# Three steps of a hybrid attention layer moved in its hand-written order: norms of the second query group, turns of mixer A's values, differences of mixer B's halves

## The chip, the core and the metric

The kernel runs on one core of a Trainium2 chip. The metric is the device time of one execution in microseconds (us). The median of the three runs shown is 924.02 us (921.49, 924.02 and 924.33).

## What is computed

The layer takes 512 tokens of width 2048, with 16 meta tokens ahead of them (528 positions). The reference, cut to what matters:

```python
hn = rmsnorm(h, pre_norm_g)
proj = einsum('bld,dc->blc', hn, w_in)
qa, ka, va, ga, qb, kb, vb, gb = split(proj)
# mixer A: 8 query heads of 128, 2 key/value heads; q and k are normed per head, then turned by rotary angles
q = axial_rope(rmsnorm(heads(qa), q_g)); k = axial_rope(rmsnorm(heads(ka), k_g))
ya = (softmax(q k^T * scale) v) * silu(ga)
# mixer B: 8 heads, a difference of two softmaxes with a distance penalty
a = softmax(s1) - lam * softmax(s2)
yb = rmsnorm(a v, sub_g) * (1 - lambda_init) * silu(gb)
y = einsum('blc,cd->bld', concat(ya, yb), w_out)
out = (h + rmsnorm(y, post_norm_g))[:, 16:]
```

## The kernel before

**Precision.** Operands are fp32. Each is split into a high part (rounded, on ScalarE, `hi`, L334) and a low part (the remainder, on VectorE, `lo`, L337), and a product is three matmuls: high by high, low by high, high by low. Weights come in chunks of 128 by 1024: loaded into `st` (L148), split into `wh` (ScalarE, L155) and `wl` (VectorE, L156), with three buffers for each of the three.

**Stages.** (1) The eight heads of mixer B: their gate, value, key and query projections, each a `dense_T` of two weight chunks, with the attention of the head before woven between the matmuls. (2) Mixer A, with two groups of four query heads. For each group there are a query projection (`queries_A`), one key head (`keys_A`) and one value head (`values`). In the order of the program: keys and values of group 0, queries of group 0, queries of group 1, then keys and values of group 1. The attention of group 0's heads is woven into the second query projection and what follows it. (3) The eight gates of mixer A, with the attention of the heads woven in. (4) The output projection, made of products of sums and differences of token halves.

**Weaving.** `Lanes` writes the order of TensorE (PE) out by hand. It keeps a clock that counts the expected time of the matmuls and transposes issued so far (`mm` charges a matmul of n columns n / 2370 us, with n at least 256). A task is a generator; `yield x` means that it goes on once this clock has advanced by x, and `poll`, called after every three matmuls of a projection, runs at most one due task that issues to PE. The lags are in `LAG`.

**Order on the other engines.** All matmuls, all transposes and the loads through `load` keep the program's order. Instructions of VectorE (DVE), ScalarE (ACT), GpSimd (POOL) and the other DMAs are ordered by the framework when the program is built: it takes what its own model of times finds ready, earlier program positions first, and may so put a ready instruction of a late position into a gap that it expects. The weight splits stand 60 positions forward (`high_priority`, L153). On the chip each engine then takes its instructions in that fixed order.

**The lines that the change and the steps of the prediction touch:**

- `values` (from L380): the projected values, scaled by `rB` into `vf` (L328, buffer tag `tT`, two buffers), are turned on PE by the task `turn`: four transposes into a PSUM tile `tr` (L63), split into `vh` and `vl`, and `LAG["bank"]` = 2.8 later the 16 meta tokens (`vm`). The task starts `LAG["vals"]` = 3.5 after the projection.
- `tr`, with two PSUM buffers in all, also takes the transposes of the probabilities `p` (L447 to 463: two of four blocks, read by `ph` on ACT and `pl` on DVE, and a small one read by `pm`), of queries (`qn`), of keys (`kfA`, `kn`, `km`) and the products with the values (`pv`). A transposition waits on PE until the buffer's last reader is done.
- attention of a head of mixer A: scores into `sc` (one PSUM tile), scaled and copied with the maximum by DVE (L600), exponentials by ACT (L603), reciprocal by DVE (L604), scaling by POOL (L605), then `p_times_v`.
- `queries_A`: four PSUM tiles copied into `qn` (ACT, L704), then the task `turn` (L707 to 713): for each of the four token blocks `head_norm` (four squares with sums on ACT, L622; POOL's `rstd`, L247 and L249; four scalings on DVE, L625) and `rope` (five operations on DVE, L635 to L640, through a tile `t2` with tag `tT`), then `yield LAG["norm"]` = 4.0, for both groups.
- `keys_A`: the keys, copied into `kfA` (ACT, L646, tag `tT`), turned, normed and roped (`kn`, `km`), and turned back (`kh`, `kl`), by the lags 3.5, 2.8, 10.2 and 2.8.
- `half_dead` (L869): at k = 8 of the last gate's projection, when the tiles of x for k below 8 are dead, mixer B's gated outputs are split into the operands of the first two output products: `b0` (first token half) and `t1` (second half minus first half). The halves are loaded by `come` (L862) into `ob` tiles that lie in buffers of the tags `ql`, `f` and `tT`. The four differences are L877; the splits into `ah`, `al` (b0) and `bh`, `bl` (t1) follow.
- `splits` lists the pairs (`wh`, `wl`) of the weight splits as they were written. At `half_dead` two later chunks have been fetched ahead, so `splits[-3]` is the second chunk of the last gate and `splits[-4]` its first.

Of the kernel before, what the change touches and what calls it, by code (L numbers as in the profile page):

```python
# [29 lines left out]


LAG = dict(vals=3.5, bank=2.8, bankA=1.5, bankB=2.5, turnA=1.5, turnB=1.5, pvA=2.6, pvB=4.0, scB=3.0,
           pB=8.0, ss=6.0, qA=2.35, scA=5.4, pA=4.14, rope=10.2, head=3.85, fin=1.35, qn=1.4, norm=4.0)

AHEAD = -60

# [4 lines left out]
class Lanes:  # L41
# [13 lines left out]
    def mm(self, out, lhsT, rhs, start, stop, **kw):  # L55
        n = int(np.prod(rhs.shape[1:]))
        us = max(n, 256) / 2370.0
        if rhs.dtype == F32:
            us = 4 * max(n, 128) / 2370.0
        self._add(self.nc.tensor.matmul(out, lhsT, rhs, start=start, stop=stop, **kw), us)  # L60

    def transpose(self, out, in_, ident):
        self._add(self.nc.tensor.transpose(out, in_, ident), 0.109)  # L63
# [42 lines left out]
def kernel(ctx: ExitStack, tc: tile.TileContext, xT, xn, xm, w_s, w_t, w_q, w_o,  # L106
                             gpre, gq, gk, lams, gsub, gpost, ident_d, cos_d, sin_d, dist_d, out):
    nc = tc.nc
    lanes = Lanes(tc)
# [50 lines left out]
    splits = []  # L160
# [31 lines left out]
    KEYS = [(0, HALF), (HALF, NT)]  # L192
    REAL = [(NM, NT)]

    def three(ps, wh, wl, k, n0, n1):
        mm(ps, wh, xh[k][:, n0:n1], start=(k == 0), stop=False)
        mm(ps, wh, xl[k][:, n0:n1], start=False, stop=False)
        mm(ps, wl, xh[k][:, n0:n1], start=False, stop=(k == KT - 1))
# [4 lines left out]
    def fetch(ahead=2):  # L203
        while todo and len(chunks) <= ahead:
            src = todo.pop(0)
            chunks.append(src() if callable(src) else wload(src))
        return chunks.pop(0)

    def dense_T(segs, pss=None, half=None):

        pss = pss or [pd.tile([P, 512], F32, name="pd", tag="pd") for _ in segs]
        for k0 in range(0, KT, 8):
            wh, wl = fetch()
            for k in range(k0, k0 + 8):
                c = slice((k - k0) * P, (k - k0 + 1) * P)
                for (n0, n1), ps in zip(segs, pss):
                    three(ps[:, :n1 - n0], wh[:, c], wl[:, c], k, n0, n1)
                    lanes.poll()
                if half and k == 8:
                    half()  # L220
        return pss
# [38 lines left out]
    for t in (TT, 0, 1, 2, 3):  # L260
        rows = P if t < TT else NM
        src = xn[t * P:(t + 1) * P, :] if t < TT else xm
        for j in range(2 if t < 2 else 4):

            tag, w = ("pl", "ph")[j % 2], 1024
            if t >= 2:
                tag, w = ("f", "g", "ql")[t - 2], 512
            st = (gp if tag == "g" else ap).tile([P, w], F32, name="xns", tag=tag,
                                                 bufs=2 if t < 2 else 4)[:rows]
# [56 lines left out]
    def halves(pss, dst):  # L326
        for (n0, n1), ps in zip(KEYS, pss):
            nc.vector.tensor_tensor(out=dst[:, n0:n1], in0=ps[:, :n1 - n0], in1=rB[:, n0:n1],  # L328
                                    op=ALU.mult)
# [3 lines left out]
    def hi(dst, src):  # L333
        nc.scalar.activation(dst, src, AF.Copy)  # L334

    def lo(dst, src, h):
        nc.vector.tensor_tensor(out=dst, in0=src, in1=h.bitcast(F32), op=ALU.subtract)  # L337
# [39 lines left out]
            lo(l2[L], qf[U], q2[U])  # L377
        return (q1, l1), (q2, l2)

    def values(pss):  # L380

        vf = ap.tile([P, NT], F32, name="vf", tag="tT")
        halves(pss, vf)
        vh = ap.tile([P, TT, P], F32R, name="vh", tag="vh")
        vl = ap.tile([P, TT, P], F32R, name="vl", tag="vl")
        vm = ap.tile([96, P], F32R, name="vm", tag="vm")
        nc.vector.memset(vm.bitcast(F32), 0.0)

        def turn():
            yield from whole()  # L390
            tr = ptr.tile([P, 512], F32, name="tr", tag="tr")
            for c in range(TT):
                transpose(tr[:, c * P:(c + 1) * P], vf[:, NM + c * P:NM + (c + 1) * P], ident)
            tv = tr.rearrange("p (c d) -> p c d", d=P)
            hi(vh, tv)
            lo(vl, tv, vh)
            yield LAG["bank"]
            yield from whole()
            tr = ptr.tile([P, 512], F32, name="tr", tag="tr")
            transpose(tr[:NM, :P], vf[:, 0:NM], ident)  # L400
            hi(vm[0:NM], tr[0:NM, :P])
            hi(vm[64:64 + NM], tr[0:NM, :P])
            lo(vm[32:32 + NM], tr[0:NM, :P], vm[0:NM])

        return (vh, vl, vm), lanes.spawn(turn(), LAG["vals"])

    def gate(pss, name):
        g = gp.tile([P, SEQ], F32, name=name, tag="g", bufs=4)
# [8 lines left out]
    def whole():  # L417

        while pv_open[0]:
            yield 0.1  # L420
# [196 lines left out]
    def head_norm(raw, n, g, rows=P):  # L617

        ss = ap.tile([P, 4], F32, name="ssh", tag="ssh", bufs=4)
        for i in range(n):  # L620
            jk = ap.tile([P, P], F32, name="jk", tag="jk", bufs=1)
            nc.scalar.activation(jk[:rows], raw[:, i, :], AF.Square, accum_out=ss[:rows, i:i + 1])  # L622
        rstd(ss[:rows, :n], ss[:rows, :n], P, rows)
        for i in range(n):
            nc.vector.scalar_tensor_tensor(out=raw[:, i, :], in0=raw[:, i, :],  # L625
                                           scalar=ss[:rows, i:i + 1], in1=g[:rows], op0=ALU.mult,
                                           op1=ALU.mult)
# [56 lines left out]
    def queries_A(g, before=None):  # L684

        pss = [pd.tile([P, 512], F32, name="pd", tag="pd") for _ in range(TT)]
        for k0 in range(0, KT, 2):
            wh, wl = fetch()

            for k, ts in [(k, h) for h in ((0, 1), (2, 3)) for k in (k0, k0 + 1)]:  # L690
                c = slice((k - k0) * 512, (k - k0 + 1) * 512)
                for t in ts:
                    ts_ = slice(NM + t * P, NM + (t + 1) * P)
                    mm(pss[t], xh[k][:, ts_], wh[:, c], start=(k == 0), stop=False)
                    mm(pss[t], xl[k][:, ts_], wh[:, c], start=False, stop=False)
                    mm(pss[t], xh[k][:, ts_], wl[:, c], start=False, stop=(k == KT - 1))
                    lanes.poll()
        if before:
            before()
        res = []  # L700
        for t in range(TT):
            tag = "ql" if g == 0 else "fr" if t < 2 else "f"
            qn = ap.tile([P, 4, P], F32, name="qn", tag=tag, bufs=2 if tag == "fr" else 4)
            nc.scalar.activation(qn.rearrange("p n d -> p (n d)"), pss[t], AF.Copy,  # L704
                                 scale=rt[:, t:t + 1])
            res.append(qn)

        def turn():
            for t, qn in enumerate(res):
                head_norm(qn, 4, gqB)  # L710
                rope(qn, cosT[:, t:t + 1].broadcast_to([P, 4, 2, 32]),
                     sinT[:, t:t + 1].broadcast_to([P, 4, 2, 32]))
                yield LAG["norm"]

        return res, lanes.spawn(turn(), 0.0)


# [37 lines left out]
    def otile(name, n, dt=F32R):  # L755
        return xtile(name, n, dt)[:, NM:NT]
# [23 lines left out]
    pss = dense_T(KEYS, [sc[:, 0, :], sc[:, 1, :]], spread)  # L780
# [10 lines left out]
    with behind():  # L791
        lambdas()
    v = values(pss)
    with behind():
        gB = [gate(first[2], "gB0")] + [None] * (NH - 1)
# [6 lines left out]
    for h in range(NH):  # L802
# [6 lines left out]
        if h + 1 < NH:  # L809
            if h:  # L810
                weigh(2)
            pss = dense_T(KEYS)
# [8 lines left out]
    def start_heads(grp, qn, q_task, k, v):  # L821
        for h in range(4 * grp, 4 * grp + 4):
            heads[NH + h] = lanes.spawn(attention_A(h, qn, q_task, *k, *v), LAG["qn"],
                                        q_task if h == 0 else heads[NH + h - 1])

    pss = dense_T(KEYS)
    finish_head(NH - 2)
    kA = keys_A(pss)
    vA = values(dense_T(KEYS))

    def zeros():
        finish_head(NH - 1)
# [3 lines left out]
    start_heads(0, *queries_A(0, zeros), kA, vA)  # L836
    second_q = queries_A(1)
    kA = keys_A(dense_T(KEYS))
    start_heads(1, *second_q, kA, values(dense_T(KEYS)))
    assert not steps and not adds  # L840

    NP = TT // 2 * P
# [1 line left out]
    TTv, SUB, ADD = nc.vector.tensor_tensor, ALU.subtract, ALU.add  # L844
# [5 lines left out]
    def split(tiles, src):  # L850
        h, l = tiles
        hi(h, src)
        lo(l, src, h)
# [11 lines left out]
    def two_(t):  # L865
        return t.rearrange("p (i q) -> p i q", i=2)
# [3 lines left out]
    def half_dead():  # L870
        for to, n in ((b0, 0), (t1, 8)):
            for i in range(4):
                st, sd = of_B[2 * i:2 * i + 2]
                to.append([two_(otile(f"{'ab'[n // 8]}{x}{i}", n + 2 * i + j))
                           for j, x in enumerate("hl")])
                if n:
                    TTv(out=sd, in0=st, in1=sd, op=SUB)  # L877
                    st = sd
                split(to[i], st)

# [285 lines left out]
```

## Time and profile before

The profile shows one execution of 921.97 us, whose span from the first to the last instruction is 920.2 us.

| what | value |
|---|---|
| device time, median of 3 | 924.02 us |
| device time of the profiled execution | 921.97 us |
| its span | 920.2 us |
| mean granted TensorE clock | 0.996 |
| busy: PE / DVE / ACT / POOL | 901.2 / 588.4 / 503.4 / 122.0 us |
| DMA | 149.86 MB, mean 163 GB/s |

In the trace group 0's keys and values are projected up to 474.6 us (`vf` of group 0), its queries up to 518 us, the queries of group 1 up to 567.6 us, the keys of group 1 up to 597.6 us and its values up to 617.5 us. The gates follow up to 755 us, and the output projection up to the end.

Times in rows are in us from the span's start, and mean durations in ns where that is said. A row of the timeline has the start, the duration, the engine, the line, the operation, what it writes and reads, and in brackets how long the engine had stood idle before it and who released it. PE's busy time contains the overlap of pipelined matmuls, so its rows are longer than the distance of their starts.

### The profile page before, as it was taken

How to read it: one execution, taken by the hardware profiler on the slowest of the kernel's cores; microseconds unless marked ns; L12 is line 12 of the kernel's file. 1: busy time of each engine (PE TensorE's matmuls, PEld its weight loads, DVE VectorE, ACT ScalarE, POOL GpSimd, SP SyncE). 2: the span in 40 equal slices, each digit the busy share in tenths (PEclk: the TensorE clock that was granted, in tenths of full speed). 3: DMA queues.
4: the chain of work that ended last, by engine and by line, in shares of the span. 5: the costliest groups of instructions: out<-in, count | busy, mean ns of one | idle time of the engine just before them, and what ended most of it. 6: DMA issues, size and time to landing. Idle time of an engine off the chain costs nothing.

```text
span 920.2 us, 14275 instructions
## 1 busy us (share of the span) xinstructions
PE 901.2 (98%) x5450; PEld 798.7 (87%) x5450; DVE 588.4 (64%) x1041; ACT 503.4 (55%) x877; POOL 122.0 (13%) x168
## 2 busy tenths in 40 slices
PE   9999999999999999999999999998999999999995
PEld 8999898998989899898988888887888888888884
DVE  6676675747557485665764464856555565876887
ACT  6564564737455474654753535555556564665452
POOL 0102110210201111111020101321111100000012
PEclk9999999999999999999999999999999999999998
DMA  9837646664848568475223232133122228889784
GB/s 341 286 120 210 173 124 157 184 195 135 224 119 236 134 180 217 119 224 131 80 70 103 76 107 69 47 109 109 62 77 92 63 87 300 274 284 314 251 250 177
DMA packets 52980, 149.86 MB, mean 163 GB/s; under 512 B 7921, under 2 KB 14961, under 8 KB 52529
## 3 DMA queue, kind: packets, MB, share of 16 engines
q1 hardware_dynamic: 48160, 132.18, 42.3%
q0 software_dynamic: 4608, 16.78, 10.6%
q8 instruction: 42, 0.69, 0.3%
q14 instruction: 26, 0.20, 0.1%
q10 hardware_dynamic: 144, 0.01, 0.0%
HBM read 140.55 MB, written 41.94 MB: 198 GB/s over the span
## 4 chain that ended last, share of the span: by engine, by line
PE 87%; DVE 7%; ACT 2%; DMA 2%; issue 1%; POOL 0%; SPq 0%; DVEq 0%; ACTq 0%; POOLq 0%
PE pd L60 58%; PE po L60 14%; PE sc L60 6%; PE pv L60 5%; PE tr L63 4%; DVE wl L156 1%; DVE y L1064 1%; DMA st<-in_w_s_dram 1%; DVE p L600 1%; DMA ob<-oscr 1%; DMA st<-in_w_o_dram 0%; DVE pl L337 0%; ACT p L603 0%; PE ss L60 0%; DVE y L988 0%
## 5 line engine op out<-in xcount | busy, mean ns | idle before, releaser
L60 PE MATMUL pd<-xh,wh 128*128 128x264 f32 (+1 forms) x992 | 333.4, 336 | 0.0
L60 PE MATMUL pd<-xh,wl 128*128 128x264 f32 (+1 forms) x992 | 323.1, 326 | 0.2
L60 PE MATMUL pd<-xl,wh 128*128 128x264 f32 (+1 forms) x992 | 323.0, 326 | 0.0
L155 ACT ACTIVATE wh<-st 128x1024 fp32r<-128x1024 f32 (+2 forms) x159 | 165.6, 1042 | 205.6 <-PE pd L60 81.0
L156 DVE TENSOR_TENSOR wl<-st,wh 128x1024 fp32r<-128x1024 f32 (+2 forms) x159 | 191.2, 1203 | 102.6 <-ACT wh L155 101.6
L60 PEld LDWEIGHTS pd<-xh,wl 128*128 128x128 f32 x992 | 186.4, 188 | 16.7 <-DVE wl L156 0.6
L60 PEld LDWEIGHTS pd<-xh,wh 128*128 128x128 f32 x992 | 186.8, 188 | 11.1 <-ACT wh L155 0.3
L60 PEld LDWEIGHTS pd<-xl,wh 128*128 128x128 f32 x992 | 187.2, 189 | 9.5
L509 ACT ACTIVATE p<-p,mx 128x528 f32<-128x528 f32 x64 | 47.0, 734 | 43.2 <-DVE mx L501 42.9
L63 PE MATMUL tr<-ident,p 128*128 128x128 f32 (+1 forms) x320 | 50.7, 272 | 3.9 <-DVE pl L337 3.1
L337 DVE TENSOR_TENSOR pl<-tr,ph 128x512 fp32r<-128x512 f32 x64 | 43.3, 685 | 16.6 <-ACT ph L334 16.2
L501 DVE CUSTOM_DVE_ANT_0 p<-sc,dist 128x528 f32<-128x528 f32 x64 | 44.8, 700 | 11.5 <-PE sc L60 11.1
L60 PE MATMUL pd<-wh,xh 128*128 128x512 f32 x128 | 51.1, 399 | 0.0
L60 PE MATMUL pd<-wl,xh 128*128 128x512 f32 x128 | 50.0, 390 | 0.0
L60 PE MATMUL pd<-wh,xl 128*128 128x512 f32 x128 | 49.9, 390 | 0.0
L63 PEld LDWEIGHTS tr<-ident,p 128*128 128x128 f32 (+1 forms) x320 | 36.5, 131 | 15.3 <-DVE pl L337 3.7
L334 ACT ACTIVATE ph<-tr 128x512 fp32r<-128x512 f32 x64 | 37.6, 590 | 22.3 <-PE tr L63 21.8
L603 ACT ACTIVATE p<-p,mxA 128x528 f32<-128x528 f32 x32 | 23.5, 735 | 41.4 <-DVE mxA L600 41.4
L516 DVE SCALAR_TENSOR_TENSOR p<-p,c 128x528 f32<-128x528 f32 x32 | 24.5, 766 | 30.8 <-POOL p L514 30.8
L461 POOL TENSOR_SCALAR pm<-pm 32x256 fp32r<-32x256 f32 x32 | 22.8, 712 | 149.1 <-ACT pm L334 148.6
L605 POOL TENSOR_SCALAR p<-p,smA 128x528 f32<-128x528 f32 x32 | 23.1, 722 | 145.7 <-DVE smA L604 110.9
L749 POOL DMA_DIRECT2D ws<-in_w_o_dram x32 | 26.7, 836 | 118.0 <-DMA ws<-in_w_o_dram 64.7
(221 smaller groups left out, 1591.5 us busy)
## 6 DMA issues: line engine op xcount, KB each, us to landing
st<-in_w_t_dram SPq DMA_DIRECT2D x82, 512.0 KB, 4.2
ws<-in_w_o_dram POOLq DMA_DIRECT2D x32, 512.0 KB, 8.4
st<-ws SPq DMA_DIRECT2D x32, 512.0 KB, 4.0
st<-in_w_o_dram SPq DMA_DIRECT2D x24, 512.0 KB, 4.4
ws<-in_w_o_dram SPq DMA_DIRECT2D x16, 512.0 KB, 5.7
ws<-ws SPq DMA_DIRECT2D x16, 512.0 KB, 5.1
st<-in_w_q_dram SPq DMA_DIRECT2D x16, 512.0 KB, 3.5
xs<-in_xT_dram SPq DMA_DIRECT2D x16, 264.0 KB, 5.5
```

The lines of the kernel that those rows point to most:

```text
L60: self._add(self.nc.tensor.matmul(out, lhsT, rhs, start=start, stop=stop, **kw), us)
L63: self._add(self.nc.tensor.transpose(out, in_, ident), 0.109)
L155: splits.append((nc.scalar.activation(wh[:, c], st[:, c], AF.Copy), nc.vector.tensor_tensor(out=wl[:, c], in0=st[:, c], in1=wh[:, c].bitca ...
L156: nc.vector.tensor_tensor(out=wl[:, c], in0=st[:, c], in1=wh[:, c].bitcast(F32), op=ALU.subtract)))
L334: nc.scalar.activation(dst, src, AF.Copy)
L337: nc.vector.tensor_tensor(out=dst, in0=src, in1=h.bitcast(F32), op=ALU.subtract)
L501: nc.vector.tensor_tensor_reduce(out=two(p), in0=sc[:, :, :HALF], in1=two(dist[:, w0:w0 + NT]), scale=-0.125 / slope(h), scalar=3.0e38, op ...
L509: nc.scalar.activation(p2[m], p2[m], AF.Exp, scale=-1.0, bias=mx[:, m:m + 1], accum_out=sm[:, m:m + 1])
L516: nc.vector.scalar_tensor_tensor(out=p2[0], in0=p2[1], scalar=c2, in1=p2[0], op0=ALU.mult, op1=ALU.add)
L603: nc.scalar.activation(p, p, AF.Exp, scale=-1.0, bias=mx, accum_out=sm)
L605: nc.gpsimd.tensor_scalar(out=p, in0=p, scalar1=sm, scalar2=1.0, op0=ALU.mult, op1=ALU.mult)
L749: nc.gpsimd.dma_start(out=dst, in_=src, accum_op=ALU.add)
```

## The change

- Group 1's norms go in steps of 9.0 on the clock of `Lanes` in place of 4.0; group 0's stay at 4.0.
- The values of mixer A, both groups, are turned 7.0 after their projection in place of 3.5; those of mixer B stay at 3.5.
- The four differences of mixer B's halves are put behind the low part of the last gate's first weight chunk in DVE's order.

```diff
-           pB=8.0, ss=6.0, qA=2.35, scA=5.4, pA=4.14, rope=10.2, head=3.85, fin=1.35, qn=1.4, norm=4.0)
+           pB=8.0, ss=6.0, qA=2.35, scA=5.4, pA=4.14, rope=10.2, head=3.85, fin=1.35, qn=1.4, norm=(4.0, 9.0), valsA=7.0)
...
-    def values(pss):
+    def values(pss, lag="vals"):
...
-        return (vh, vl, vm), lanes.spawn(turn(), LAG["vals"])
+        return (vh, vl, vm), lanes.spawn(turn(), LAG[lag])
...
-                yield LAG["norm"]
+                yield LAG["norm"][g]
...
-    vA = values(dense_T(KEYS))
+    vA = values(dense_T(KEYS), "valsA")
...
-    start_heads(1, *second_q, kA, values(dense_T(KEYS)))
+    start_heads(1, *second_q, kA, values(dense_T(KEYS), "valsA"))
...
                 if n:
-                    TTv(out=sd, in0=st, in1=sd, op=SUB)
+
+                    with tc.issue_after(splits[-4][1].ins):
+                        TTv(out=sd, in0=st, in1=sd, op=SUB)
                     st = sd
                 split(to[i], st)
```

## The prediction

> **What bounds the kernel.** I read the page first. TensorE (PE) is busy nearly throughout, so only its gaps can be won: an edit elsewhere pays as far as PE waits less.
>
> ```profile
> span 920.2 us, 14275 instructions
> ...
> PE 901.2 (98%) x5450; PEld 798.7 (87%) x5450; DVE 588.4 (64%) x1041; ACT 503.4 (55%) x877; POOL 122.0 (13%) x168
> ```
>
> Next the busy times by stretches of 20 us (columns: stretch, sum, then busy time of PE, PEld, DVE, ACT, POOL, then PEclk), around the second query group and in the gates.
>
> ```profile
> 580.00:600.00 20.00, 17.92 (x148) 17.27 (x147) 16.78 (x42) 10.06 (x27) 6.10 (x9) 1.00 0.09 28
> 600.00:620.00 20.00, 18.25 (x145) 17.36 (x144) 11.62 (x29) 10.37 (x29) 5.25 (x9) 1.00 0.33 105
> 620.00:640.00 20.00, 17.85 (x103) 14.45 (x101) 12.67 (x24) 8.78 (x18) 3.50 (x4) 1.00 0.31 106
> ...
> 720.00:740.00 20.00, 20.00 (x116) 17.09 (x115) 10.11 (x20) 11.47 (x19) 3.62 (x5) 1.00 0.23 77
> ```
>
> PE loses 2.08, 1.75 and 2.15 us in 580 to 640, while DVE is at its fullest in the first of these; in 720 to 740 it loses nothing. Third, PE's waits from 563 to 645 us in groups (total, times, longest), and the three longest in the timeline:
>
> ```profile
> PE tr L63 <- DVE pl L337: 3.8, 6, 1.8
> PE tr L63 <- DVE kl L337: 1.9, 1, 1.9
> PE tr L63 <- ACT oA L610: 0.5, 1, 0.5
> ...
> 587.48 0.39 PE L63 MATMUL tr<-ident,p 128*32 128x128 f32 x2 [1.79 <-DVE pl L337]
> ...
> 601.16 0.66 PE L63 MATMUL tr<-ident,kfA 128*128 128x128 f32 x4 [0.78 <-DVE pl L337]
> ...
> 624.36 0.66 PE L63 MATMUL tr<-ident,vf 128*128 128x128 f32 x4 [1.85 <-DVE kl L337]
> ```
>
> All are transposes waiting for one of the two `tr` buffers, whose reader is late. Together they are 6.2 us; that is the most that this change can win here.
>
> **The norms in steps of nine.** The wait at 587.48 has this chain (last matmul of the scores, DVE, then ACT, then DVE):
>
> ```profile
> 580.76 0.28 PE L60 MATMUL sc<-kh,qlA 128*128 128x264 f32 x1
> ...
> 582.11 0.35 DVE L625 SCALAR_TENSOR_TENSOR qn<-qn,ssh,gqB 128x128 f32<-128x128 f32 x1 [1.00 <-POOL ssh L249]
> ...
> 584.59 0.70 DVE L600 CUSTOM_DVE_ANT_0 p<-sc,zed 128x528 f32<-128x528 f32 x1
> ...
> 585.39 0.73 ACT L603 ACTIVATE p<-p,mxA 128x528 f32<-128x528 f32 x1 [3.44 <-DVE mxA L600]
> ...
> 586.12 0.57 ACT L334 ACTIVATE ph<-tr 128x512 fp32r<-128x512 f32 x1
> ...
> 586.74 0.69 DVE L337 TENSOR_TENSOR pl<-tr,ph 128x512 fp32r<-128x512 f32 x1
> ```
>
> The scores end at 581.04, but DVE copies them only at 584.59: norm and rope operations stand ahead, one of which holds the line 1.00 us for POOL. The exponential waits for the copy, `ph` stands behind the exponential on ACT, `pl` behind `ph`, and PE behind `pl`. What the four norm steps cost:
>
> ```profile
> L625 DVE SCALAR_TENSOR_TENSOR qn<-qn,ssh,gqB 128x128 f32<-128x128 f32 x16 | 5.2, 366 | 3.3 <-POOL ssh L249 3.3
> ...
> L639 DVE TENSOR_TENSOR qn<-qn,cosT 128x256 f32<-128x256 f32 x8 | 3.1, 414 | 0.0
> L640 DVE TENSOR_TENSOR qn<-qn,t 128x512 f32<-128x512 f32 x4 | 2.8, 690 | 0.1
> L635 DVE SCALAR_TENSOR_TENSOR t<-qn,sinT 128x256 f32<-128x256 f32 x4 | 2.1, 527 | 0.0
> L637 DVE TENSOR_TENSOR t<-qn,sinT 128x256 f32<-128x256 f32 x4 | 1.7, 413 | 0.0
> ...
> L622 ACT ACTIVATE jk<-qn 128x128 f32<-128x128 f32 x16 | 4.9, 308 | 0.4
> ```
>
> That is 14.9 us of DVE, 3.7 a step. Neither number nor size changes, only their places. The task starts when the last query matmul is written, and the keys end here:
>
> ```profile
> 567.64 0.69 ACT L704 ACTIVATE qn<-pd,rt 128x512 f32<-128x512 f32 x1 [1.13 <-PE pd L60]
> ...
> 597.64 0.66 ACT L646 ACTIVATE kfA<-pd 128x264 f32<-128x264 f32 x2
> ...
> 607.25 1.14 DVE L625 SCALAR_TENSOR_TENSOR kn<-kn,ssh,gkB 128x128 f32<-128x128 f32 x4 [3.83 <-POOL ssh L249]
> ...
> 617.48 0.99 DVE L328 TENSOR_TENSOR vf<-pd,rB 128x264 f32<-128x264 f32 x2
> ```
>
> Steps two to four stood at about 572, 576 and 580, all ahead of the scores of 580.15; now they stand at about 577, 587 and 597 (the hand-written clock runs a little short of the trace). At 581 only step two precedes the copy. Without step three's share in 582.11 to 584.59 (its 1.00 of waiting and its scalings, 0.35 and 0.34) and with step two's rope no longer split by it, the copy comes 1.5 to 3 us earlier, and the wait shrinks by as much: between 0 (the later positions are filled in early again) and 1.79; I take 1.5, the lower end of what the line clears. What is late next: step four, once done by 596, falls near 600. It can use the 3.83 us that DVE idles before 607.25, but 601.16 already shows 0.78 of waiting for a `pl`. I charge 0.5 for it (bounds 0 and one more wait like that, 0.78). The four heads that need these queries start after the values, so the end of the task, four steps of nine, some 39 us after 567.6 or about 606, delays nobody: the first of them begins after 617. Cost there 0; without that cover each us late would be one on PE.
>
> **The differences.** The wait at 624.36:
>
> ```profile
> 618.44 0.28 PE L60 MATMUL sc<-kh,qlA 128*128 128x264 f32 x1
> ...
> 620.59 0.69 DVE L877 TENSOR_TENSOR ob<-ob 128x512 f32<-128x512 f32 x1 [2.12 <-DMA ob<-oscr]
> 621.20 0.70 DVE L600 CUSTOM_DVE_ANT_0 p<-sc,zed 128x528 f32<-128x528 f32 x1
> ...
> 622.00 0.74 ACT L603 ACTIVATE p<-p,mxA 128x528 f32<-128x528 f32 x1 [2.03 <-DVE mxA L600]
> ...
> 622.74 0.58 ACT L334 ACTIVATE kh<-tr 128x512 fp32r<-128x512 f32 x1
> ...
> 623.03 0.67 DVE L877 TENSOR_TENSOR ob<-ob 128x512 f32<-128x512 f32 x1
> 623.62 0.68 DVE L337 TENSOR_TENSOR kl<-tr,kh 128x512 fp32r<-128x512 f32 x1
> ```
>
> A difference that is written in the last gate stands here in DVE's order, and waits 2.12 us for its DMA while the scores behind it have been ready since 618.72. Taken away, copy, exponential, `kh` and `kl` all come about 2 us earlier, `kl` ends near 622 in place of 624.2, and the transposes that wanted the buffer at 622.5 don't wait: 1.85 won (bounds 1.2, if `kl` finds DVE at another 0.67 operation, and 1.85). Their new place:
>
> ```profile
> L877 DVE TENSOR_TENSOR ob<-ob x4: 673/686/693, 620.6 to 632.9; 128x512 f32<-128x512 f32 x4
> ...
> 725.15 1.23 DVE L156 TENSOR_TENSOR wl<-st,wh 128x1024 fp32r<-128x1024 f32 x1
> ...
> 733.10 1.22 DVE L156 TENSOR_TENSOR wl<-st,wh 128x1024 fp32r<-128x1024 f32 x1 [2.04 <-ACT wh L155]
> ...
> 739.58 0.69 DVE L560 TENSOR_TENSOR gt<-pd,rB 128x512 f32<-128x512 f32 x1 [1.87 <-PE pd L60]
> ...
> 745.13 0.62 ACT L334 ACTIVATE bh<-ob 128x512 fp32r<-128x512 f32 x1
> ```
>
> The last gate's first chunk is the `wl` of 725.15 (its buffer is freed three chunks ahead of its use at 739). Four times 0.69, 2.8 us, must fit between there and 745, where their first reader stands; the data came 100 us before, so nothing waits behind them for a DMA. DVE is free for half of 720 to 740 (10.11 busy of 20). I take 0; the other end is one operation ahead of a `pl`, 0.69. The DMAs stay unmoved. If that cover failed, the output products that need the splits start after 755, a reserve of 10 us.
>
> **The values.** Turning them 3.5 later changes PE's order, not its amount. At 624.36 the four transposes come right after those of `kn` and `p`; later, they find the buffers freer. With the differences gone there is little left to win, and the places around have waits of 0.3 to 0.8. I take 0, from -0.5 to 0.78. Their later end frees a `tT` buffer some 3 us later, for which the last `ob` load waits in SP's queue; the weight load behind it serves a chunk some 14 us ahead of its use (as 725.15 stands to 739.58), so this is covered. Group 0's values, turned near 480, are costed the same way: 0.
>
> **The sum.** 1.5 + 1.85 - 0.5 = 2.85 won, and 0.4 of the 1.2 that four short waits for `pl` hold (3.8 - 1.79 - 0.78), since the long ones were each followed by a short one: 3.3 us. Against the profiled execution's own 921.97 (span 920.2 and 1.8 around it) that gives 918.7. That execution lies low among the runs shown, so against the median of 924.02 I predict 920.7.
>
> On the clock, the stretches with all these waits have PEclk 1.00, so a wait costs its own length. The Trainium skill (TensorE: Matmul & The Clock Gate, "A second HAM failure mode: psum-queue depth-cycling") says that short idles between groups of matmuls that cycle PSUM buffers can let the clock oscillate between half and full. By it each long wait would also cost half of a window of about 3.4 us, an estimate from that page, and removing two would win 3.4 more; the trace shows no such drop.
>
> **The rivals.**
>
> *The norms do not move.* The framework fills gaps by what it expects to be ready, as L877 at 620 instead of 750 proves. If it puts steps three and four early again, or the wait at 587 only moves to 601, the differences alone pay: 1.85, a median of 922.2. For it: DVE idled 3.3 us in all before `qn` scalings, so it expects them earlier than they come. Against it: at 581 the copy and step three contend, and now the copy has the earlier place.
>
> *More goes.* The six waits hang together; if nearly all go, 5.5 us: a median of 918.5. For it: one late copy feeds each chain; against it: the wait for `oA` (0.5) and those of 601 to 611 have the keys' own norm in front, which stays.
>
> *Slower: step four takes a `tT` buffer ahead of `kfA`.* There are two; `kfA`'s copy at 597.64 would wait if steps three and four hold both. Step four, from 597 on, needs 1.2 of ACT (4.9 / 4), 1.0 for POOL (the wait at 582.11) and 3.7 of DVE, the last drawn out to some 9 where DVE is 58% busy with other work (11.62 of 20): `kfA` at 608 and its transposes about 609, or 607 as all comes 1.8 earlier without the wait at 587, instead of 601.2. Less the 1.85 won behind it this is 4 us slower: 926.0 for the profiled execution, 928.0 for the median. It decides if step four's rope is placed before 597. Against it: step three should be over by 592.
>
> **How the numbers follow.** My forecast has 0.55, the unmoved norms 0.27, more gone 0.10, the slower case 0.08. A difference of 0.3%, 2.8 us, is about what a measurement of this kernel can tell from no change. Four fifths of the forecast's chance lies above 2.8 won, which with "more goes" gives 0.53 faster; slower 0.08; the rest, 0.39, same. The range: below, 5.5 won and a little of the runs' own spread, 917.8; above, the unmoved norms with 1.85 won, and 2.2 more for the runs' spread and a new wait (0.78), 924.4.
>
> **What the profile would show.** Right: no difference (L877) before 725; no DVE wait on `ob` at 620; the transposes of `vf` some 3 us after those of `kn` without a long wait; steps of `qn` scalings about 9 us apart, and the copy of the scores within 1.5 us after they end; PE's idle time in 580 to 640 near 2.7 us instead of 6. Wrong: `qn` scalings bunched as before, a wait of over 1 us on PE between 595 and 612, `kfA` copied late, or new waits on PE in 725 to 750.

## The result, and the profile after

The changed kernel takes 918.83 us (median of 7 runs, 917.87 to 921.08), the kernel before in the same comparison 922.85 us (median of 7, 921.49 to 924.53). The ratio is 0.995 with a 95% interval of 0.9936 to 0.9965, so 3.2 to 5.9 us are won. The profiled execution took 918.62 us, with a span of 916.8 us against 920.2.

The busy times of the changed kernel by stretches (columns as before):

```profile
580.00:600.00 20.00, 18.01 (x150) 17.56 (x149) 14.68 (x36) 9.10 (x23) 4.87 (x7) 1.00 0.12 41
600.00:620.00 20.00, 19.38 (x152) 18.26 (x151) 15.84 (x41) 12.10 (x39) 6.87 (x11) 1.00 0.32 92
620.00:640.00 20.00, 20.00 (x115) 16.61 (x114) 10.74 (x22) 10.90 (x20) 2.75 (x4) 1.00 0.43 143
...
720.00:740.00 20.00, 20.00 (x115) 17.13 (x114) 13.12 (x23) 13.33 (x22) 3.61 (x5) 1.00 0.25 73
```

PE's idle time in 580 to 640 is 2.6 us (1.99 + 0.62 + 0) in place of 6.0. But the first stretch is nearly as it was; all of the gain lies in the second and third. PE's two longest remaining waits there, and a new one near 482:

```profile
482.45 0.66 PE L63 MATMUL tr<-ident,vf 128*128 128x128 f32 x4 [0.73 <-DVE kl L337]
...
588.21 0.39 PE L63 MATMUL tr<-ident,p 128*32 128x128 f32 x2 [1.76 <-DVE pl L337]
...
609.74 0.39 PE L63 MATMUL tr<-ident,p 128*32 128x128 f32 x2 [0.47 <-DVE pl L337]
```

The waits of 0.78 (601), 0.51 (606), 1.85 (624), 0.30 (630) and 0.27 (642) are gone, 3.7 us; the wait of 1.8 near 588, of which the prediction wanted 1.5, is there. Its chain on DVE after the change:

```profile
582.84 0.35 DVE L625 SCALAR_TENSOR_TENSOR qn<-qn,ssh,gqB 128x128 f32<-128x128 f32 x1 [1.00 <-POOL ssh L249]
583.11 0.42 DVE L635 SCALAR_TENSOR_TENSOR t<-qn,sinT 128x256 f32<-128x256 f32 x1
583.45 0.42 DVE L637 TENSOR_TENSOR t<-qn,sinT 128x256 f32<-128x256 f32 x1
583.78 0.75 DVE L639 TENSOR_TENSOR qn<-qn,cosT 128x256 f32<-128x256 f32 x2
584.45 0.34 DVE L625 SCALAR_TENSOR_TENSOR qn<-qn,ssh,gqB 128x128 f32<-128x128 f32 x1
584.72 0.68 DVE L640 TENSOR_TENSOR qn<-qn,t 128x512 f32<-128x512 f32 x1
585.32 0.70 DVE L600 CUSTOM_DVE_ANT_0 p<-sc,zed 128x528 f32<-128x528 f32 x1
```

It is the old chain, one of step three's scalings waiting 1.00 us for POOL included. What did move is step three's rope and the whole of step four. Before, step four's rope ended right ahead of another copy of scores, and after the change that copy waits for the scores alone. DVE before:

```profile
595.02 0.69 DVE L640 TENSOR_TENSOR qn<-qn,t 128x512 f32<-128x512 f32 x1
595.63 0.70 DVE L600 CUSTOM_DVE_ANT_0 p<-sc,zed 128x528 f32<-128x528 f32 x1
```

And DVE after:

```profile
594.59 0.71 DVE L600 CUSTOM_DVE_ANT_0 p<-sc,zed 128x528 f32<-128x528 f32 x1 [1.03 <-PE sc L60]
```

DVE after, near 620: no difference stands ahead of the copy any more, and `kl` ends at 621.65 in place of 624.3.

```profile
618.35 0.71 DVE L600 CUSTOM_DVE_ANT_0 p<-sc,zed 128x528 f32<-128x528 f32 x1
...
620.96 0.69 DVE L337 TENSOR_TENSOR kl<-tr,kh 128x512 fp32r<-128x512 f32 x1 [0.69 <-ACT kh L334]
```

One loss of the changed kernel is not among the waits. Step four's rope now runs on DVE from 613.1 to 616.3, ahead of the copy of the scores that end near 613.8. Behind that copy stands `qlA`, which the next scores read:

```profile
615.60 0.68 DVE L640 TENSOR_TENSOR qn<-qn,t 128x512 f32<-128x512 f32 x1
616.20 0.70 DVE L600 CUSTOM_DVE_ANT_0 p<-sc,zed 128x528 f32<-128x528 f32 x1
616.82 0.68 DVE L337 TENSOR_TENSOR qlA<-tr,qh 128x512 fp32r<-128x512 f32 x1
...
617.05 0.36 PE L60 MATMUL sc<-kh,qh 128*128 128x264 f32 x1
...
617.56 0.39 PE L60 MATMUL sc<-kh,qlA 128*128 128x264 f32 x1
```

The first of these scores starts 0.24 us behind the matmul ahead of it in place of 0.12, and from it to the matmul behind the six scores it takes 1.10 us (617.05 to 618.15) in place of 0.73 (617.84 to 618.57 in the kernel before). So 0.5 us are lost here.

The differences (L879 now) run here, with PE at 20.00 of 20 in that stretch:

```profile
L879 DVE TENSOR_TENSOR ob<-ob x4: 682/686/695, 723.2 to 726.3; 128x512 f32<-128x512 f32 x4
```

### The profile page after: what moved, and what is told of

The parts are those of the page before. It is cut to its first block, busy times and chain, and to the rows that moved or that the text cites. A ratio compares the mean times of both kernels' runs of the same rounds, so it can differ in the third digit from the quotient of the medians.

```text
span 916.8 us, 14275 instructions
## 1 busy us (share of the span) xinstructions
PE 900.9 (98%) x5450; PEld 799.4 (87%) x5450; DVE 588.7 (64%) x1041; ACT 503.3 (55%) x877; POOL 121.7 (13%) x168
## 4 chain that ended last, share of the span: by engine, by line
PE 91%; DVE 5%; ACT 2%; issue 1%; DMA 1%; POOL 0%; DVEq 0%; ACTq 0%; POOLq 0%
PE pd L60 60%; PE po L60 14%; PE sc L60 6%; PE pv L60 5%; PE tr L63 5%; DVE wl L156 1%; DVE y L1066 1%; DMA st<-in_w_o_dram 1%; PE hot L60 0%; PE ss L60 0%; DVE y L990 0%; ACT wh L155 0%; ACT jk L622 0%; DVE l L337 0%; ACT p L603 0%
## 5 line engine op out<-in xcount | busy, mean ns | idle before, releaser
L514 POOL TENSOR_SCALAR p<-p,sm 128x528 f32<-128x528 f32 x32 | 23.4, 730 | 138.7 <-DVE sm L511 127.7
```

Of the source, the lines that this page charges most:

```text
L514: nc.gpsimd.tensor_scalar(out=p2[0], in0=p2[0], scalar1=sm[:, 0:1], scalar2=1.0, op0=ALU.mult, op1=ALU.mult)
```

## The experiments

**How they are compared.** Whole spans scatter by about 2 us for reasons away from the change: over the twelve profiles, the first transposes of group 0's keys (`kfA`) start between 461.66 and 463.95 us, and from the first output product (`po`) to the end it takes 164.42 to 165.86, with no order by edit. Where two kernels have the same work, the times between marks on PE's timeline agree to a few hundredths. The table gives, from the one profiled execution of each kernel, the time in us between four marks: `kfA` (462.14 before), the first query transposes of mixer A (541.94), those of the third head (589.56), and the first output product (755.39). Ratios are those of the device times to the kernel before, run beside each, with 95% intervals; two expectations call the third mark that of the second head.

| kernel | kfA to first queries | to third head | to first product | sum | ratio |
|---|---|---|---|---|---|
| before | 79.80 | 47.62 | 165.83 | 293.25 | 1 |
| changed | 80.45 | 47.67 | 161.47 | 289.59 | 0.995 (0.9936 to 0.9965) |
| norm alone | 79.80 | 47.64 | 163.97 | 291.41 | 0.9967 (0.9953 to 0.9981) |
| values alone | 80.46 | 47.65 | 163.64 | 291.75 | 0.9981 (0.9968 to 0.9993) |
| differences alone | 79.81 | 47.62 | 163.78 | 291.21 | 0.9968 (0.9954 to 0.9983) |
| values and differences | 80.46 | 47.65 | 162.63 | 290.74 | 0.9958 (0.9945 to 0.9971) |
| norm and differences | 79.77 | 47.63 | 162.64 | 290.04 | 0.9953 (0.9935 to 0.9971) |
| step four alone and differences | 79.80 | 47.87 | 162.45 | 290.12 | 0.9958 (0.9945 to 0.997) |
| changed, group 0's values as before | 79.80 | 47.63 | 161.36 | 288.79 | 0.9941 (0.992 to 0.9962) |
| the same, steps of thirteen | 79.80 | 46.42 | 162.37 | 288.59 | 0.994 (0.9918 to 0.9962) |
| changed, steps three and four held | 80.46 | 46.31 | 161.46 | 288.23 | 0.994 (0.9924 to 0.9956) |
| both: held, group 0's values as before | 79.80 | 46.27 | 161.35 | 287.42 | 0.9926 (0.9911 to 0.9941) |

The theory after the result: each wait hangs on one edit, and step three's scalings keep their place whatever the prediction thought of them. The rivals: only the three together work, or the values' later turn cleared the wait near 624.

### The norm alone

```diff
-... norm=4.0)
+... norm=(4.0, 9.0))
```

> Only the nine-us steps of the second queries' norm. Theory (each edit clears its own waits; step three's scalings are not moved by it, step four is): PE's wait of 1.8 us near 587 stays, those near 601 and 606 (0.78 and 0.51) go, the one near 624 (1.85) stays; idle PE time in 580 to 640 about 4.7 us, span about 1.3 us below before (919). Rival (the norm step does nothing by itself): idle 6.0 us and no gain. Rival (only all three together work): new waits of the same size, no gain.

1.84 us are won between the marks. The waits near 601 and 606 are gone and the one near 588 (1.81) stays, as the theory has it. But the wait near 624 did not stay: PE's waits there are now

```profile
621.76 0.66 PE L63 MATMUL tr<-ident,vf 128*128 128x128 f32 x4 [0.25 <-DVE kl L337]
...
628.69 0.40 PE L63 MATMUL tr<-ident,p 128*32 128x128 f32 x2 [0.98 <-DVE pl L337]
```

With DVE's order changed, the differences stand behind the copy near 618 and hold up the next one instead. DVE of the same kernel:

```profile
620.27 0.83 DVE L877 TENSOR_TENSOR ob<-ob 128x512 f32<-128x512 f32 x1 [0.58 <-DMA ob<-oscr]
...
625.19 0.69 DVE L877 TENSOR_TENSOR ob<-ob 128x512 f32<-128x512 f32 x1 [1.33 <-DMA ob<-oscr]
625.80 0.70 DVE L600 CUSTOM_DVE_ANT_0 p<-sc,zed 128x528 f32<-128x528 f32 x1
```

So what one edit wins depends on the others, by way of where the free differences land.

### The values alone

```diff
-    vA = values(dense_T(KEYS))
+    vA = values(dense_T(KEYS), "valsA")
...
-    start_heads(1, *second_q, kA, values(dense_T(KEYS)))
+    start_heads(1, *second_q, kA, values(dense_T(KEYS), "valsA"))
```

> Only the later turn of mixer A's values, both groups. Theory: the difference that waits 2.1 us for its DMA still holds the copy of the scores up, so the buffer of the turned keys still comes free near 624, and whichever transposes come next wait for it, 0.9 us or more; span between 0 and 1 us below before. Rival (the later turn alone clears the wait near 624): that wait goes wholly, 1.85 us won. In both a wait near 482 of about 0.7 in place of 0.23.

The theory's wait is there: now the small transposition of the keys stands where that of the values stood. PE of this kernel:

```profile
624.57 0.23 PE L63 MATMUL tr<-ident,km 16*128 16x16 f32 x1 [0.98 <-DVE kl L337]
```

But half of the 1.85 went, and so did the 0.30 and 0.27 behind it: 2.19 us won in the last part, 0.66 lost in group 0. The 1.50 us between the marks are more than the theory allowed (at most 1), though the wait did not go wholly, as the rival had it.

### The differences alone

```diff
-                    TTv(out=sd, in0=st, in1=sd, op=SUB)
+                    with tc.issue_after(splits[-4][1].ins):
+                        TTv(out=sd, in0=st, in1=sd, op=SUB)
```

> Only the differences put behind the gate's chunk. Theory: no DVE wait for ob near 620, the 1.85 us wait near 624 and the one of 0.3 behind it go, those near 587, 601, 606 and 610 stay; idle PE time in 580 to 640 about 3.8 us, span about 2.2 us below before (918.0). Rival (the values' turn does it): a wait of over 1 us stays near 624, under 1 us won.

2.05 us are won, all in the last part; no wait near 624 is left, those of 0.78, 0.51 and 0.45 before it stay. DVE now takes the copy as the scores end:

```profile
619.27 0.71 DVE L600 CUSTOM_DVE_ANT_0 p<-sc,zed 128x528 f32<-128x528 f32 x1 [0.29 <-PE sc L60]
```

The wait of 0.29 near 629 stays, against what the theory said; it and one of 0.27 near 641 are the values' share.

### Values and differences; norm and differences

The first of these leaves the norm at 4.0 in the changed kernel, the second leaves the values at 3.5.

> Both the later values and the moved differences, the norm left in steps of four. Theory: as the differences alone but for the values' own small effects (about 0.5 lost near 482, up to 0.5 won near 630): span 1.7 to 2.5 us below before; the waits near 587, 601 and 606 stay, since they hang on the norm steps. Rival (all of the gain near 601 and 606 came from the shift of other work, not from the norm steps): those two waits go here too, 3.4 us won.

2.51 us between the marks. The waits near 601 and 606 stand there unchanged, so they hang on the norm's steps:

```profile
603.67 0.66 PE L63 MATMUL tr<-ident,kfA 128*128 128x128 f32 x4 [0.79 <-DVE pl L337]
...
608.67 0.66 PE L63 MATMUL tr<-ident,p 128*128 128x128 f32 x4 [0.52 <-ACT oA L610]
```

> Norm steps of nine and the moved differences, values turned as before. Theory (the values' later turn adds nothing, and costs 0.5 near 482): all waits from 595 to 645 but the one near 610 gone, the 1.8 near 587 stays, 0.23 near 482; span 3.5 to 4 us below before, equal to or 0.5 below the changed kernel. Rival (the later values are needed): a wait of over 0.5 us near 620 to 630, span 1 us or more above the changed kernel.

3.21 us, so 0.45 less than with the later values: the theory held that they add nothing, and that was wrong. They win 1.17 in the last part (162.64 to 161.47), where waits of 0.29 and 0.27 go, and lose 0.68 in the first.

### Step four alone, with the differences

```diff
-                yield LAG["norm"]
+                yield 19.0 if g and t == 2 else LAG["norm"][g]
```

Here `LAG["norm"]` is (4.0, 4.0).

> Norm steps one to three of the second queries at four us as before, step four alone at 27; differences moved, values as before. Theory (step four's rope ahead of the copy of scores near 594 makes the waits near 601 and 606; step three's later rope wins nothing): the same waits as with steps of nine and the moved differences (1.8 near 588, 0.46 near 609, 0.29 and 0.27 behind), 0.78 and 0.51 gone; from the second head's query transposes to the first output product 162.6 us, span about 3.5 below before. Rival (step three's later rope is needed): the waits near 601 and 606 stay, 163.8 us.

162.45 us in the last part, the same as with all steps at nine (162.64), and no wait near 601 or 606. Step four is what the norm's edit moves to profit. The loss on the scores near 617 comes with it: 0.4 us here, 0.5 with all steps at nine, none in the two kernels that move the differences and leave all steps at four. The wait near 588 is 2.01, with step three's rope in its old place, and costs 0.24 more.

### Group 0's values as before

```diff
-    vA = values(dense_T(KEYS), "valsA")
+    vA = values(dense_T(KEYS))
```

> The changed kernel with group 0's values turned at 3.5 again, group 1's at 7.0. Theory (the wait of 0.73 near 482 comes of group 0's later turn): 0.23 there, span 0.5 us below the changed kernel (916.3). Rival (chance of the profile): 0.73 again.

79.80 us in the first part again, 0.65 less than the changed kernel, and a wait of 0.23 near 483. The span, expected at 916.3, is 917.4: this execution came to the `kfA` mark 0.6 us later and took 0.8 longer behind the last mark. In group 0 the later turn comes right behind the transposes of `kn` and `p`, and needs the buffer that `kl` is still reading. DVE of the changed kernel there, with the split of a weight chunk ahead of `kl`:

```profile
480.57 1.22 DVE L156 TENSOR_TENSOR wl<-st,wh 128x1024 fp32r<-128x1024 f32 x1 [2.30 <-ACT wh L155]
481.71 0.68 DVE L337 TENSOR_TENSOR kl<-tr,kh 128x512 fp32r<-128x512 f32 x1
```

### Steps of thirteen

```diff
-... norm=(4.0, 9.0), valsA=7.0)
+... norm=(4.0, 13.0), valsA=7.0)
```

on the kernel of the section above.

> Norm steps of thirteen us, group 1's values at 7.0, group 0's at 3.5, differences moved: only the step differs from the run with late values of group 1. Theory (step three's scalings stay ahead of the copy near 585 only because eighteen us on the hand-written clock is not late enough): the wait of 1.79 near 588 falls to about 0.43, from the first to the second head's query transposes 46.3 us in place of 47.6; step four, now near 610, may cost up to 0.8 near 616 to 624; span 1 to 2 us below that run. Rival (the scalings are put ahead whatever the step): 1.79 and 47.6 us again.

The lag does reach step three's scalings if it is long enough: the wait near 588 falls, and the second part by 1.21 us. What is won is given back later. PE:

```profile
586.52 0.39 PE L63 MATMUL tr<-ident,p 128*32 128x128 f32 x2 [0.55 <-DVE pl L337]
...
640.55 0.39 PE L63 MATMUL tr<-ident,p 128*32 128x128 f32 x2 [0.83 <-DVE pl L337]
```

The last part is 1.01 longer: 0.2 of it is lost on the scores near 615, the rest at the wait near 640 and just ahead of it. The span is 2.0 below that of the section above, as expected, but that is luck: between the marks it is 0.2, and the rest is the scatter of the start and the end.

The cause of the wait near 640 is open. Step four's last operation ends at 623.05, so no rope holds up DVE there. Ahead of this `pl` stand, on ACT, two loads of activation tables (634.73 and 637.16, 1.28 us each), the exponential (638.46) and `ph` (639.19). The kernel with steps of nine has the same loads (636.20 and 638.62), but another order on PE: the queries of the fifth head are turned at 636.88, ahead of two turns of `p`, and here at 638.42, behind them. By the program that head waits for the end of the norms' task. That this order makes the wait is likely, but no run shows it.

### Steps three and four held behind the scores

The changed kernel, with an explicit edge in DVE's order: `copies` collects the copies of scores (L600) as they are written.

```diff
-                head_norm(qn, 4, gqB)
-                rope(qn, ...)
+                with tc.issue_after(copies[-1].ins) if g and t > 1 else nullcontext():
+                    head_norm(qn, 4, gqB)
+                    rope(qn, ...)
```

> The changed kernel, with the norm and rope of steps three and four of the second queries put behind the latest copy of scores written before them, in DVE's order; that takes step three's four scalings, one of which waits 1.0 us for POOL, from ahead of the copy near 585. Theory (these scalings hold the copy up): the copy comes 1.5 us earlier, the wait of 1.76 near 588 falls below 0.5, span 1.3 to 1.9 us below the changed kernel (915.2). Rival (step two's rope alone or ACT holds it): the wait stays above 1.2, span as the changed kernel. Rival (the held work makes a new wait near 590 to 616): the gain is lost there.

The second part falls by 1.36 us. DVE, with step two's operations alone ahead of the copy and no wait for POOL among them:

```profile
583.28 0.43 DVE L635 SCALAR_TENSOR_TENSOR t<-qn,sinT 128x256 f32<-128x256 f32 x1
583.63 0.42 DVE L637 TENSOR_TENSOR t<-qn,sinT 128x256 f32<-128x256 f32 x1
583.96 0.76 DVE L639 TENSOR_TENSOR qn<-qn,cosT 128x256 f32<-128x256 f32 x2
584.75 0.69 DVE L640 TENSOR_TENSOR qn<-qn,t 128x512 f32<-128x512 f32 x1
585.36 0.70 DVE L600 CUSTOM_DVE_ANT_0 p<-sc,zed 128x528 f32<-128x528 f32 x1
```

The scores end at 583.14 (the last starts at 582.86), so the copy is 2.2 us behind them in place of 3.6 (581.76 to 585.32 in the changed kernel), and PE's wait is

```profile
588.25 0.40 PE L63 MATMUL tr<-ident,p 128*32 128x128 f32 x2 [0.42 <-DVE pl L337]
```

The diagnosis in the prediction was right, then, and only the remedy missed: the copy comes 1.4 us earlier and the wait loses 1.34, near the 1.5 of the sum. The held work makes no new wait, the last part is 161.46 in place of 161.47. The span was expected at 915.2 and is 917.5: this execution came to the `kfA` mark 1.4 us later than the changed kernel's and took 0.7 longer behind the last mark.

### Held, and group 0's values as before

> The changed kernel with group 0's values at 3.5 again and steps three and four of the second queries' norm behind the latest copy of scores. Theory: both gains add, span about 2 us below the changed kernel (914.8), 0.6% below before. Rival: no better than the changed kernel, 916.8.

The two gains add: 287.42 us between the marks, 2.17 below the changed kernel, a span of 914.3, and 916.93 us (median of 6) against 923.43 before. It is the fastest kernel here. Its waits on PE from 563 to 645 us:

```profile
PE tr L63 <- DVE pl L337: 1.1, 3, 0.5
```

## Why the prediction was right, point by point

**The total** was right: 3.3 us forecast, 3.66 measured between the marks and 4.0 between the medians. 1.2 of the 1.9 us by which 920.7 lies above 918.83 comes of the base: the median of before was 924.02 over three runs and is 922.85 over seven. The terms were not all right: the norm's steps were to win 1.0 and won 1.14 in another way, so two misses cancelled, and that the sum holds is luck.

**The differences**, 1.85 forecast: 2.05 alone. The chain (a difference waiting for its DMA, the copy behind it, the exponential, `kh`, `kl`) is shown by the run with that edit alone, and their new place costs nothing, as said. Beside the norm's steps they are worth 1.33 (163.97 to 162.64).

**The norm's steps**, 1.5 less 0.5 forecast: 1.14 beside the differences (163.78 to 162.64), from another place. The step that failed is "At 581 only step two precedes the copy". Step three's scalings stayed ahead of it with steps of nine; the wait near 588 went from 1.79 to 1.76. That part is what the rival of the unmoved norms said, and the sign of being wrong, "`qn` scalings bunched as before", is in the trace: step two's start at 580.35 and step three's at 582.84. What the prediction had no term for is the gain from step four. It had stood ahead of the copy of the scores that end near 593.8, and once moved it cleared the waits near 601 and 606: from the third mark to the transposes that had waited near 606 it takes 14.97 us in place of 16.61, so 1.64 are won up to there. The charge for step four was right in size and wrong in place: nothing new waits near 600, but 0.50 is lost on the scores near 617. The prediction had looked at where step four would go, and not at whom it was holding up where it stood.

**The short waits**, 0.4 forecast, as each long wait was followed by a short one: those of 0.30 and 0.27 went, but not with the long ones. The differences alone leave them (0.29 and 0.27), and the values' later turn takes them away. The other two, 0.23 and 0.45, stay (0.22 and 0.47).

**The values**, 0 forecast, from -0.5 to 0.78: 1.17 won in group 1 beside the other two edits and 0.68 lost in group 0, 0.5 in all. Of the 1.17 the two short waits are 0.9 by the delay of their starts (0.69 and 0.67 behind the matmul ahead, in place of 0.23); the rest is not traced. Costing group 0 "the same way" was the error: there the later place is a worse one.

**The clock, and what a wait costs.** PEclk is 1.00 in the stretches of both kernels. A wait cost a little more than "its own length", since the row ahead of it is longer than the usual distance of the starts and hides the first part of the delay. Near 624 the transposes start 2.25 us behind the matmul ahead of them in place of 0.23: 2.02 lost, of which 1.85 is shown as idle, and 2.05 came back. Near 601 and 606 the distances are 1.06 and 0.79 in place of 0.12: 1.61 lost, 1.29 shown, and 1.64 came back. The oscillation of which the Trainium skill speaks (TensorE: Matmul & The Clock Gate, "A second HAM failure mode: psum-queue depth-cycling") would have given 1.7 more for each, by the estimate in the prediction; these waits did not cause it.

**The slower rival** did not happen: `kfA` is copied at 596.61, a microsecond earlier than before.

## What to carry to other kernels

A lag or a position only ranks an instruction; where an in-order engine is filled by readiness, late work still lands ahead of urgent work, and what it then waits for (a DMA, POOL) is paid by all behind it. Tie such work by an explicit edge to the urgent instruction that it must not precede: that won here what a lag of nine did not win and a lag of thirteen gave back. Before moving a step, ask whom it holds up where it stands, as well as whom it will meet; and check each term of a sum by its own run, since a right total can hide two wrong terms.

## What the runs showed that was not expected

The same stretch of PE's timeline repeats to a few hundredths of a microsecond in different executions and even different kernels (79.77 to 79.81 us in the eight kernels that leave group 0's values in place, 80.45 to 80.46 in the four that move them), while the start (461.66 to 463.95) and the end (164.42 to 165.86) scatter by 2.3 and 1.4 us. Edits worth half a microsecond can be read between marks where whole times cannot tell them apart. The list of waits is not the whole account either: it shows too little of each wait, and it has no entry for the 0.5 us that the scores near 617 lost.
